# A block inversion in which each partition holds every fourth row, with changed prices in the planner

## The chip, the cores and the metric

The kernel runs on one core of a Trainium2 chip. The metric is device time in microseconds (us) of that core. Of the engines, PE is TensorE (matmuls; PEld is its weight load), DVE is VectorE, ACT is ScalarE, POOL is GpSimd and SP is SyncE, which here issues the DMAs.

## The reference

Two layers on a sequence of 1,024 tokens of width 1,024, all in float32. Layer 1 mixes with a gated DeltaNet (8 heads of 128), layer 2 with stick-breaking attention (8 heads of 128); each is followed by a SwiGLU feed-forward network (FFN, hidden width 2,816) and a gated per-layer embedding. What the change touches is the DeltaNet's triangular system, one per chunk of tokens and head:

```python
G = jnp.cumsum(g, axis=-1)
decay_mat = jnp.exp(jnp.where(causal, G[..., :, None] - G[..., None, :], -jnp.inf))
kk = jnp.einsum('bnhrd,bnhsd->bnhrs', k, k)
a_low = jnp.where(strict, beta[..., None] * kk * decay_mat, 0.0)
rhs = jnp.concatenate([v * beta[..., None], k * (beta * jnp.exp(G))[..., None]], axis=-1)
sol = lax.linalg.triangular_solve(a_low + eye, rhs, left_side=True, lower=True, unit_diagonal=True)
u, w = sol[..., :dv], sol[..., dv:]
...
def step(state, xs):                       # scan over the chunks
    v_new = u_c - w_c @ state
    o = q_c @ state + qk_c @ v_new
    state = state * gl_c + k_c.T @ v_new
```

The kernel uses chunks of 128 tokens, so a head has 8 unit lower triangular matrices of 128 x 128 to invert.

## The kernel before

**Numbers.** Most dense products run as three matmuls on a high and a low part of each float32 operand (`whi`, `wlo`; type float32r), 128 x 128 weights by 512 columns. Splitting weights into the two parts (ACT for `whi`, DVE or POOL for `wlo`) and evacuating PSUM are the main work of the other engines.

**Order.** No loop fixes the order of the instructions. Class `Flow` is a list scheduler that runs while the program is written. Every piece of work is a generator; `run` always resumes the one of best priority whose condition holds at the planned time, and where none can go it takes the next dense matmul from `fill`. After each instruction `issued` advances a model: a clock for each engine, the time at which each tile is written or read last, a price from `cost` for each instruction, one from `lat` for a handover between engines, and for a DMA a landing time (`rings`: its issue + 1.1 us, and bytes at 360 GB/s). A change of any price can so change the order of every later instruction on every engine. The chip then executes each engine's list in that order, and each instruction waits for its inputs. All instructions are issued in the wrapper `Engine.__getattr__`, so the profile gives line 64 for all of them; they are told apart by their tiles.

**Sequence.** Start and first projections up to about 84 us; DeltaNet with dense projections and parts of the embedding products as fill up to about 640 us; output projection; FFN from 785 to 1480 us; attention from 1480 to about 1940 us; output projection; the second FFN to the end.

**The block inversion** (`gdn_inv`, one generator per head `h`). A head's eight 128 x 128 matrices L (tile `LT`) give 8 x 4 = 32 diagonal blocks of 32 x 32 (`B` = 32). They go through DRAM (`Ld`) to tile `Ls`, in which 128 partitions hold the 32 blocks, each block in four neighbouring partitions with all of its 1,024 elements. Each of the four holds `CG` = 8 rows of the block's inverse: tile `xr` (the rows) and `yr` (products), 8 x 32 elements a partition. For s = 30 down to 0 a step multiplies columns s+1 to 31 of the rows by a row of L (`yr<-xr,Ls`) and sums the products into column s (`xr<-yr`), 62 DVE instructions a head. The start values of `xr` and `yr` are unit rows from `masks`, which `const_table` makes. Then `xr` is stored to `Xd` and the blocks are loaded back (`X<-Xd`, four loads) into the diagonal of 128 x 128 matrices, and matmuls (`products`) complete the full inverse `Z`. The next head's `Ls` is loaded only after this head's last step (mark `("x", h)`).

**Around it.** `gdn_prep` makes `QK`, `qf`, `kf`, `vt` per unit (half a head's chunks); it loads `eGb`, a row of decays copied to all partitions, into a tile with one buffer. `Gb` is a load of the same kind. `gdn_rec` is the recurrence over chunks, with tiles `vin`, `vn`, `vE`, `Sm` and PSUM banks `rc`, `r`, `po`. `ple_products` writes embedding products (`<-Z,whi`, `<-ou,whi` in the start) into the banks `po`, `rc`, `r`, `mm`; ACT or DVE clear them into `sg` or `ca`, and these are stored with `ppD<-sg`, `ppD<-ca`. In attention, `z` are scores, `c` their cumulative sums (from `sh`, `sl` by `triR`), `zs` the scores in SBUF, `wh` and `wl` the parts of the weights, and `o` the output.

Of the kernel before, what the change touches and what calls it, by code (L numbers as in the profile page):

```python
# [11 lines left out]
ALU = mybir.AluOpType  # L12
# [3 lines left out]
P = 128  # L16
# [15 lines left out]
B = 32  # L32
NB = P // B
CG = 8
# [3 lines left out]
def const_table():  # L38

    i = np.arange(P)  # L40
    r, c = i[:, None], i[None, :]
    tab = [b.astype(np.float32) for b in (r == c, r <= c, r >= 0 * c, r >= c, r < c)]
    tab.append((r // B > c // B).astype(np.float32))
    g = i[:, None, None] % (B // CG)
    e = np.arange(B)[None, None, :] == CG * g + np.arange(CG)[None, :, None]
    tab += list(e.reshape(P, 2, P).astype(np.float32).transpose(1, 0, 2))
    return np.ascontiguousarray(np.stack(tab, 1))

# [34 lines left out]
class Flow:  # L83
# [30 lines left out]
    def cost(self, eng, op, out, ins, kw):  # L114
        n = 1
        for d in (ins[0] if op == "tensor_reduce" else out).shape[1:]:
            n *= d
        psum = any(x.space == PSUM for x in ins)
        if eng == "pe":
            if op != "transpose" and ins[0].dtype == F32R:  # L120
                return max(n, P) / 2400.0 + 0.0127
            return max(n, P) * (2 if op == "transpose" else 4) / 2400.0 + (0.003 if op == "transpose" else 0.0107)
        if eng == "dve":
            if op == "memset":
                return 0.06 + n / 3840.0
            tail = 0.06 if any(x.shape[-1] == 1 for x in ins) and n > 1 else 0.0
            if any(x.shape[-1] > 1 and x.ap[-1][0] > 1 for x in ins):
                tail += 0.085
            fast = op in ("tensor_copy", "tensor_scalar") and not psum
            return 0.069 + tail + n / (1920.0 if fast else 960.0)  # L130
        if eng == "act":
            us = (0.052 if psum else 0.094) + n / 1200.0
            return us + 0.093 * (len(ins) - 1) + (0.235 if "accum_out" in kw else 0.0)
        if op == "tensor_tensor":
            return 0.295 + 0.166 * n if kw.get("op") == ALU.pow else 0.148 + n * 0.002104
        return 0.4 + n / 1400.0 if op == "affine_select" else 0.1 + n / 1085.0

    def shared(self, eng, op, outs, ins, kw, t, c):

# [22 lines left out]
    def issued(self, eng, op, args, kw):  # L162
        aps = [x for x in list(args) + list(kw.values()) if hasattr(x, "space")]
        if not aps:
            if op == "preload_act_table_set":
                self.table = 3
            return
        outs = [kw["out"] if "out" in kw else aps[0]]
        if "accum_out" in kw:
            outs.append(kw["accum_out"])  # L170
        ins = [x for x in aps if not any(x is o for o in outs)]
        t = self.clock[eng]
        if eng == "pe":
            t = max(t, self.now)
        spans = []
        for x, w in [(o, True) for o in outs] + [(i, False) for i in ins]:
            if x.space == DRAM:
                lo, dims = x.offset, x.ap
            else:
                dims, step = x.ap[1:], x.ap[0][0]  # L180
                lo = x.offset % step if step else x.offset
            hi = lo + 1 + sum((c - 1) * d for d, c in dims)
            rec = self.mem.get(x.name)
            if rec is None:
                rec = self.mem[x.name] = {}
                old = self.old.pop(x.name, None)
                if old is not None and old in self.mem:
                    t = max([t] + [max(v[0] + self.lat(v[1], eng), v[2] + self.lat(v[3], eng)) for v in self.mem.pop(old).values()])
            for (l, h), v in rec.items():
                if l < hi and lo < h:  # L190
                    if not (w and eng == v[1]):
                        t = max(t, v[0] + self.lat(v[1], eng))
                    if (w or x.space == PSUM) and v[3] != eng:
                        t = max(t, v[2] + self.lat(v[3], eng))
            spans.append((rec, (lo, hi), w))
        if eng == "dma":
            n = 4
            for d in outs[0].shape:
                n *= d
            run = min(x.ap[-1][1] if x.ap[-1][0] == 1 else 1 for x in outs + ins)  # L200
            n *= max(1, P // run)
            self.clock["dma"] = t + 0.475
            self.rings = max(self.rings, t + 1.1) + n / 360e3
            end = self.rings
        else:
            c = self.cost(eng, op, outs[0], ins, kw)
            f = [x for x in args if isinstance(x, AF)]
            if f and f[0] in TABLES and TABLES[f[0]] != self.table:
                self.table = TABLES[f[0]]
                t += 1.4  # L210
            if eng in ("dve", "pool"):
                t = self.shared(eng, op, outs, ins, kw, t, c)
            end = t + c
            self.clock[eng] = end
            if eng == "pe":
                self.now = end
        for rec, key, w in spans:
            v = rec.setdefault(key, [-1e9, eng, -1e9, eng])
            if w:
                v[0], v[1] = end, eng  # L220
            elif end > v[2]:
                v[2], v[3] = end, eng
        self.ready = max(self.ready, end + self.LAT[eng])

    def lat(self, a, b):
        if b == "pe":
            return {"pe": 0.0, "dma": 1.2}.get(a, 0.25)
        return 0.13 if a == b and a != "dma" else self.LAT[a]

    def run(self, fill):  # L230
        test = None
# [40 lines left out]
class Net:  # L272
# [679 lines left out]
    def gdn_inv(self, h):  # L952

        nc, flow = self.nc, self.flow
# [37 lines left out]
        rk, rinv, rkb, brk2, rkE, t = (sc[:, i] for i in range(6))  # L992
# [17 lines left out]
        Ld, Xd = self.Ld[h % 2], self.Xd[h % 2]  # L1010
# [8 lines left out]
        for i, u in enumerate(us):  # L1019
            e = slice(4 * i, 4 * i + 4)  # L1020
# [2 lines left out]
        yield  # L1023
        yield lambda: h == 0 or ("x", h - 1) in flow.at
        Ls = self.g("Ls", (P, B * B))
        src = Ld.rearrange("c b s r -> (c b) (s r)").unsqueeze(1).to_broadcast([8 * NB, B // CG, B * B])
        nc.sync.dma_start(Ls, src)

        x = self.g("xr", (P, CG, B))
        y = self.g("yr", (P, CG, B))  # L1030
        rows = self.masks[:, 1:].rearrange("p a (j s) -> p (a j) s", s=B)
        nc.scalar.copy(x[:, :, B - 1], rows[:, :, B - 1])
        nc.scalar.copy(y[:, :, : B - 1], rows[:, :, : B - 1])
        yield
        Lv = Ls.rearrange("p (s r) -> p s r", r=B)
        for s in range(B - 2, -1, -1):
            nc.vector.tensor_tensor(y[:, :, s + 1 :], x[:, :, s + 1 :], Lv[:, s, s + 1 :].unsqueeze(1).to_broadcast([P, CG, B - 1 - s]), op=ALU.mult)
            yield
            nc.vector.tensor_reduce(x[:, :, s], y[:, :, s:], axis=mybir.AxisListType.X, op=ALU.add)
            yield  # L1040
        flow.mark(("x", h))
        nc.sync.dma_start(Xd.rearrange("c b r k -> (c b r k)").rearrange("(p n) -> p n", p=P), x.rearrange("p j s -> p (j s)"))
        yield
        yield lambda: h == 0 or ("w", us[0] - 1) in flow.at
        for b in range(NB):
# [1023 lines left out]
def layout(inputs):  # L2069
# [14 lines left out]

    a = {}
    a["cst"] = const_table()
    a["xT"] = np.ascontiguousarray(g["x"][0].T).reshape(NK, P, S)
    a["pT"] = np.ascontiguousarray(g["p"][:, 0].transpose(0, 2, 1)).reshape(2, 2, P, S)
# [41 lines left out]
```

## Time and profile before

| | us |
|---|---|
| median of 3 runs | 2787.19 (2784.03 to 2788.08) |
| profiled execution, its time | 2787.44 |
| its span in the trace | 2785.7 |
| PE busy | 2741.7 (98%) |
| weight load busy | 2278.1 (82%) |
| DVE busy | 1951.7 (70%) |
| ACT busy | 1324.3 (48%) |
| POOL busy | 860.4 (31%) |

The mean granted clock of PE is 0.996 of full speed. Busy times of different engines overlap. A row of the timeline view gives the start, the duration, the engine, line, operation, output<-inputs, shapes and count, and in brackets how long the engine had idled and what ended that. A row of a group gives total time, then the mean in ns. Queues of SP are written SPq.

### The profile page before, as it was taken

The page shows a single profiled execution, that of the slowest core. Times are in us where ns is not written, and L with a number is a line of the kernel's source. Part 1 is how long each engine was busy: PE and PEld are TensorE (multiplying, and loading weights), DVE is VectorE, ACT ScalarE, POOL GpSimd, SP SyncE. Part 2 cuts the span into 40 slices and gives each one's busy share as a digit, 9 for nine tenths or more (in the row PEclk, how much of TensorE's full clock was granted, in tenths as well). Part 3 has the DMA queues.
Part 4 walks back from the last instruction along what each step waited for, and adds up shares of the span by engine and source line. Part 5 has one row for each costly group of instructions (what it writes and reads, how often), then busy time and mean ns, then how long its engine had stood idle before and what let it go on. Part 6 is the DMA issues. An engine that isn't in the chain of part 4 may idle for free.

```text
span 2785.7 us, 37779 instructions
## 1 busy us (share of the span) xinstructions
PE 2741.7 (98%) x13203; PEld 2278.1 (82%) x13203; DVE 1951.7 (70%) x3733; ACT 1324.3 (48%) x2701; POOL 860.4 (31%) x742
## 2 busy tenths in 40 slices
PE   9999999999999999999999999999999999999999
PEld 8788888888778888888778888888878888888777
DVE  7687887873875665477857778887686565557783
ACT  6655555543433344322335778877443343322241
POOL 0111111100166667444101222221036666643400
PEclk9999999999999999999999999999999999999999
DMA  4412222247334444587232111114514444487623
GB/s 147 143 58 76 75 82 74 74 151 244 140 110 159 155 155 144 223 328 304 106 131 99 54 50 61 54 58 158 200 57 156 150 148 151 144 311 284 262 90 105
DMA packets 165072, 394.85 MB, mean 142 GB/s; under 512 B 34000, under 2 KB 35344, under 8 KB 155408
## 3 DMA queue, kind: packets, MB, share of 16 engines
q1 hardware_dynamic: 164880, 392.43, 39.5%
q8 instruction: 104, 1.70, 0.2%
q14 instruction: 88, 0.72, 0.1%
HBM read 273.77 MB, written 118.59 MB: 141 GB/s over the span
## 4 chain that ended last, share of the span: by engine, by line
PE 86%; DVE 7%; ACT 4%; issue 2%; DMA 1%; POOL 1%; ACTq 0%; POOLq 0%
PE dn L64 38%; PE mm L64 34%; PE tp L64 4%; PE z L64 3%; PE c L64 2%; PE o L64 2%; DVE x L64 1%; PE po L64 1%; PE rc L64 1%; PE r L64 1%; DVE u L64 1%; ACT junk L64 1%; ACT L64 1%; DVE v L64 1%; PE st L64 1%
## 5 line engine op out<-in xcount | busy, mean ns | idle before, releaser
L64 PE MATMUL mm<-x,whi 128*128 128x512 f32 x2848 | 939.0, 400 | 8.7 <-DVE x L64 5.4
L64 PEld LDWEIGHTS mm<-x,whi 128*128 128x128 f32 x2848 | 528.5, 189 | 106.7 <-DVE x L64 7.9
L64 PE MATMUL mm<-x,wlo 128*128 128x512 f32 x1424 | 568.5, 399 | 0.0
L64 PE MATMUL dn<-x,whi 128*128 128x512 f32 x1776 | 548.7, 390 | 1.8 <-DVE x L64 0.9
L64 POOL TENSOR_TENSOR wlo<-raw,whi 128x512 fp32r<-128x512 f32 x236 | 345.5, 1485 | 442.7 <-ACT whi L64 413.2
L64 ACT CAST whi<-raw 128x1024 fp32r<-128x1024 f32 x231 | 242.8, 1051 | 447.4 <-DVE raw L64 244.7
L64 PEld LDWEIGHTS dn<-x,whi 128*128 128x128 f32 x1776 | 333.3, 188 | 73.3 <-DVE x L64 2.6
L64 PE MATMUL dn<-x,wlo 128*128 128x512 f32 x888 | 345.7, 389 | 0.0
L64 PEld LDWEIGHTS mm<-x,wlo 128*128 128x128 f32 x1424 | 269.0, 189 | 46.4 <-issue 0.3
L64 PE MATMUL dn<-hx,whi 128*128 128x512 f32 x864 | 267.4, 390 | 0.4 <-DVE hx L64 0.2
L64 DVE TENSOR_TENSOR tt<-u,tt 128x512 fp32r<-128x512 f32 x140 | 143.9, 1028 | 81.5 <-ACT tt L64 81.5
L64 PEld LDWEIGHTS dn<-x,wlo 128*128 128x128 f32 x888 | 166.7, 188 | 34.4
L64 PEld LDWEIGHTS dn<-hx,whi 128*128 128x128 f32 x864 | 162.8, 189 | 35.0 <-DVE hx L64 0.6
L64 DVE TENSOR_TENSOR v<-v,dn 128x512 f32<-128x512 f32 x112 | 76.5, 684 | 155.4 <-PE dn L64 155.0
L64 DVE TENSOR_TENSOR wlo<-raw,whi 128x512 fp32r<-128x512 f32 x226 | 153.9, 693 | 27.2 <-ACT whi L64 26.9
L64 PE MATMUL dn<-hx,wlo 128*128 128x512 f32 x432 | 169.1, 391 | 3.4 <-POOL wlo L64 3.4
L64 POOL TENSOR_TENSOR wlo<-sw,whi 128x512 fp32r<-128x512 f32 x102 | 144.3, 1431 | 2.0 <-ACT whi L64 2.0
L64 ACT CAST tt<-u 128x512 fp32r<-128x512 f32 x140 | 84.8, 619 | 123.5 <-DMA yD<-tt 100.2
L64 DVE TENSOR_TENSOR E<-E,dn 128x512 f32<-128x512 f32 x132 | 90.0, 684 | 71.4 <-PE dn L64 69.1
L64 POOL TENSOR_TENSOR rs<-ms,nhalf 128x4 f32<-128x4 f32 x11 | 12.3, 1122 | 330.7 <-DVE ms L64 330.7
L64 PE MATMUL dn<-y,whi 128*128 128x512 f32 x352 | 108.4, 389 | 0.0
L64 DVE SCALAR_TENSOR_TENSOR ca<-xe,conv,ca 128x512 f32<-128x512 f32 x144 | 106.2, 744 | 0.9 <-ACT ca L64 0.4
(376 smaller groups left out, 5124.8 us busy)
## 6 DMA issues: line engine op xcount, KB each, us to landing
yD<-tt SPq DMA_DIRECT2D x296, 256.0 KB, 2.4
x<-yD SPq DMA_DIRECT2D x58, 1024.0 KB, 11.3
raw<-f_s SPq DMA_DIRECT2D x84, 512.0 KB, 3.7
raw<-d_s SPq DMA_DIRECT2D x40, 512.0 KB, 5.9
raw<-w_in SPq DMA_DIRECT2D x33, 512.0 KB, 4.0
hx<-yD SPq DMA_DIRECT2D x16, 1024.0 KB, 14.5
x<-oD SPq DMA_DIRECT2D x26, 512.0 KB, 5.8
raw<-g_out SPq DMA_DIRECT2D x16, 512.0 KB, 5.2
```

The source lines that it names most:

```text
L64: r = issue(*args, **kw)
```

## The change

- **Layout.** The four copies of a block now lie 32 partitions apart: partition p belongs to block p mod 32, and with g = p // 32 it holds rows g, g+4, g+8 and so on. `const_table` makes the unit rows for this.
- **Fewer elements.** At step s only rows that reach past column s have anything to sum. With interleaved rows these are the last 8 - j of each partition, j = (s + 1) // 4, and multiply and sum run over these alone. The count of instructions stays.
- **Ls.** Its load runs over the four copies outermost, then 32 blocks, then 1,024 elements; before it was 32 blocks, four copies, 1,024 elements.
- **Start values.** ACT copies the 256 elements of `masks` to `xr` and to `yr` (before 8 and 248 of them).
- **Xd.** It is stored by four DMAs of 32 partitions in pieces of 128 bytes, instead of one DMA of 1 KB per partition.
- **Prices.** A short f32r matmul costs at least 0.1 us (before 0.066 at 128 columns), POOL's tensor_tensor a little more, affine_select less (0.252 instead of 0.491 us at 128 elements), a DMA whose source repeats over partitions (`Gb`, `eGb`, and by its new address list `Ls`) lands 2.5 us instead of 1.1 us after issue beside its bytes, and DVE hands over to itself in 0.06 instead of 0.13 us.

```diff
-    g = i[:, None, None] % (B // CG)
-    e = np.arange(B)[None, None, :] == CG * g + np.arange(CG)[None, :, None]
+    g = i[:, None, None] // (8 * NB)
+    e = np.arange(B)[None, None, :] == g + B // CG * np.arange(CG)[None, :, None]
...
-                return max(n, P) / 2400.0 + 0.0127
+                return max(n / 2400.0 + 0.0127, 0.1)
...
-            return 0.295 + 0.166 * n if kw.get("op") == ALU.pow else 0.148 + n * 0.002104
-        return 0.4 + n / 1400.0 if op == "affine_select" else 0.1 + n / 1085.0
+            return 0.295 + 0.166 * n if kw.get("op") == ALU.pow else 0.169 + n * 0.002125
+        return 0.119 + n / 960.0 if op == "affine_select" else 0.1 + n / 1085.0
...
+            spread = any(x.ap[0][0] == 0 for x in ins)
             self.clock["dma"] = t + 0.475
-            self.rings = max(self.rings, t + 1.1) + n / 360e3
+            self.rings = max(self.rings, t + (2.5 if spread else 1.1)) + n / 360e3
...
-        return 0.13 if a == b and a != "dma" else self.LAT[a]
+        return {"dve": 0.06, "dma": self.LAT["dma"]}.get(a, 0.13) if a == b else self.LAT[a]
...
-        src = Ld.rearrange("c b s r -> (c b) (s r)").unsqueeze(1).to_broadcast([8 * NB, B // CG, B * B])
+        src = Ld.rearrange("c b s r -> (c b) (s r)").unsqueeze(0).to_broadcast([B // CG, 8 * NB, B * B])
...
-        nc.scalar.copy(x[:, :, B - 1], rows[:, :, B - 1])
-        nc.scalar.copy(y[:, :, : B - 1], rows[:, :, : B - 1])
+        nc.scalar.copy(x, rows)
+        nc.scalar.copy(y, rows)
...
-            nc.vector.tensor_tensor(y[:, :, s + 1 :], x[:, :, s + 1 :], Lv[:, s, s + 1 :].unsqueeze(1).to_broadcast([P, CG, B - 1 - s]), op=ALU.mult)
+            j = (s + 1) // (B // CG)
+            nc.vector.tensor_tensor(y[:, j:, s + 1 :], x[:, j:, s + 1 :], Lv[:, s, s + 1 :].unsqueeze(1).to_broadcast([P, CG - j, B - 1 - s]), op=ALU.mult)
...
-            nc.vector.tensor_reduce(x[:, :, s], y[:, :, s:], axis=mybir.AxisListType.X, op=ALU.add)
+            nc.vector.tensor_reduce(x[:, j:, s], y[:, j:, s:], axis=mybir.AxisListType.X, op=ALU.add)
...
-        nc.sync.dma_start(Xd.rearrange("c b r k -> (c b r k)").rearrange("(p n) -> p n", p=P), x.rearrange("p j s -> p (j s)"))
+        xd = Xd.rearrange("c b (j g) k -> g (c b) j k", g=B // CG)
+        for g in range(B // CG):
+            nc.sync.dma_start(xd[g], x[g * 8 * NB : (g + 1) * 8 * NB])
```

The set of PE's matmuls and the counts of DVE, ACT and POOL instructions stay the same. SP issues 24 more stores of Xd, and 3 more DMAs because one attention output is spilled to DRAM instead of being taken over directly. PE's order is the same up to the start of the DeltaNet, in the first FFN, and from the end of attention on.

Three places of the order follow; a row gives the line, operation, output<-inputs and output shape, names with running numbers. First, SP's queue where the first head's `Ls` and the two `eGb` are loaded, before:

```order
L64 DMA Ld_92<-LT_915 32x8x32 x4
L64 DMA Ls_983<-Ld_92 128x1x1024
L64 DMA eGb_989<-gD 128x512
L64 DMA eGb_996<-gD 128x512
L64 DMA ppD<-sg_974 128x512
L64 DMA raw_1069<-w_in 128x1024
L64 DMA ppD<-sg_1060 128x512
```

and now:

```order
L64 DMA Ld_92<-LT_913 32x8x32 x4
L64 DMA Ls_984<-Ld_92 128x1x1024
L64 DMA eGb_990<-gD 128x512
L64 DMA eGb_997<-gD 128x512
L64 DMA ppD<-sg_972 128x512
L64 DMA ppD<-sg_1065 128x512
L64 DMA raw_1083<-w_in 128x1024
```

Ls, both eGb and the first store keep their places; only a weight load (`raw`) and a store change places behind them.

Second, DVE in the same place, from the last piece of work ahead of the first step of the inversion to the reader of the first `eGb`, before:

```order
L64 TENSOR_TENSOR wlo_951<-raw_790,whi_950 128x512
L64 TENSOR_TENSOR yr_986<-xr_985,Ls_983 128x8
L64 TENSOR_REDUCE xr_985<-yr_986 128x8
L64 SCALAR_TENSOR_TENSOR QK_1025<-tp_172_1008,sc_815,Gb_724 128x128 x4
L64 SCALAR_TENSOR_TENSOR ca_965<-xe_910,conv,ca_965 128x512
L64 SCALAR_TENSOR_TENSOR ca_970<-xe_948,conv,ca_970 128x512
L64 TENSOR_TENSOR wlo_951<-raw_790,whi_950 128x512
L64 TENSOR_TENSOR yr_986<-xr_985,Ls_983 128x8x2
L64 SCALAR_TENSOR_TENSOR QK_1036<-tp_174_1018,sc_815,Gb_725 128x128 x4
L64 TENSOR_TENSOR qf_601<-qf_601,eGb_989 128x512
```

and now:

```order
L64 TENSOR_TENSOR wlo_937<-raw_795,whi_936 128x512
L64 SCALAR_TENSOR_TENSOR QK_1024<-tp_172_1009,sc_816,Gb_721 128x128 x4
L64 TENSOR_TENSOR yr_987<-xr_986,Ls_984 128x1
L64 TENSOR_REDUCE xr_986<-yr_987 128x1
L64 TENSOR_TENSOR yr_987<-xr_986,Ls_984 128x2
L64 SCALAR_TENSOR_TENSOR QK_1037<-tp_174_1019,sc_816,Gb_722 128x128 x4
L64 SCALAR_TENSOR_TENSOR ca_969<-xe_894,conv,ca_969 128x512
L64 SCALAR_TENSOR_TENSOR ca_976<-xe_964,conv,ca_976 128x512
L64 TENSOR_TENSOR wlo_937<-raw_795,whi_936 128x512
L64 TENSOR_REDUCE xr_986<-yr_987 128x1
L64 TENSOR_TENSOR qf_601<-qf_601,eGb_990 128x512
```

The first four QK updates went ahead of the first step, which has 1 x 1 elements a partition where it had 8 x 1; the reader of eGb stays behind the first steps.

Third, PE at the end of attention, from the last `z` of 128 x 128 on (`mm` is fill), before:

```order
L64 MATMUL z_3650_18777<-qh_18524,kl_18321 128x128
L64 MATMUL o_18563<-wh_18788,vh_18105 128x512
L64 MATMUL o_18563<-wl_18790,vh_18105 128x512
L64 MATMUL o_18563<-wh_18788,vl_18106 128x512
L64 MATMUL z_3658_18803<-qh_18524,kh_18320 128x256
L64 MATMUL z_3658_18803<-ql_18525,kh_18320 128x256
L64 MATMUL z_3658_18803<-qh_18524,kl_18321 128x256
L64 MATMUL c_3659_18807<-sh_18797,triR 128x128
L64 MATMUL c_3659_18807<-sl_18801,triR 128x128
L64 MATMUL c_3659_18807<-sh_18797,triR 128x128
L64 MATMUL c_3659_18807<-sl_18801,triR 128x128
L64 MATMUL mm_18534<-x_18204,whi_18322 128x512 x2
```

and now:

```order
L64 MATMUL z_3653_18812<-qh_18586,kl_18347 128x128
L64 MATMUL mm_18596<-x_18236,whi_18348 128x512
L64 MATMUL z_3659_18834<-qh_18586,kh_18346 128x256
L64 MATMUL z_3659_18834<-ql_18587,kh_18346 128x256
L64 MATMUL z_3659_18834<-qh_18586,kl_18347 128x256
L64 MATMUL c_3660_18838<-sh_18829,triR 128x128
L64 MATMUL c_3660_18838<-sl_18832,triR 128x128
L64 MATMUL mm_18596<-x_18236,whi_18348 128x512
L64 MATMUL mm_18596<-x_18236,wlo_18349 128x512
L64 MATMUL mm_18629<-x_18236,whi_18444 128x512
L64 MATMUL c_3660_18838<-sh_18829,triR 128x128
L64 MATMUL c_3660_18838<-sl_18832,triR 128x128
```

The three `o` products that stood behind this z now stand ahead of its three matmuls (not in the rows), and single fill products stand between z and the `c` products.

## The prediction

> **What bounds the kernel now.** I read the page's first lines, then a table of stretches, then the idle times in front of matmuls, then the rows of the inversion.
>
> ```profile
> span 2785.7 us, 37779 instructions
> PE 2741.7 (98%) x13203; PEld 2278.1 (82%) x13203; DVE 1951.7 (70%) x3733; ACT 1324.3 (48%) x2701; POOL 860.4 (31%) x742
> PE 86%; DVE 7%; ACT 4%; issue 2%; DMA 1%; POOL 1%; ACTq 0%; POOLq 0%
> ```
>
> PE is busy for 98% of the span and carries 86% of the chain that ended last. The change gives PE the same matmuls of the same sizes. So only the 44 us in which PE idles, the stretches of lower clock, and new waits can move the time; fewer DVE elements are worth nothing by themselves.
>
> ```profile
> 84.00:116.00 32.00, 26.22 (x145) 21.56 (x145) 21.80 (x80) 22.47 (x68) 3.70 (x4) 1.00 0.40 135
> 116.00:640.00 524.00, 520.26 (x3043) 442.07 (x3042) 407.39 (x1197) 285.52 (x809) 52.55 (x66) 1.00 0.28 89
> 785.00:1480.00 695.00, 689.25 (x3058) 569.28 (x3057) 453.85 (x642) 244.18 (x339) 327.20 (x233) 1.00 0.50 183
> 1480.00:1930.00 450.00, 449.79 (x2251) 375.09 (x2250) 353.81 (x744) 347.60 (x852) 91.59 (x152) 1.00 0.22 74
> 1930.00:1945.00 15.00, 13.18 (x52) 10.62 (x51) 11.57 (x25) 9.97 (x21) 2.68 (x5) 0.77 0.21 74
> ```
>
> Columns: stretch, length, busy time of PE, weight loads, DVE, ACT, POOL, then PE's clock, DMA share, GB/s. The new order touches the DeltaNet (84 to 640) and attention (1480 to 1945); the FFN of 785 to 1480 and everything behind 1945 keep their matmul order. In the touched stretches PE idles 32.00 - 26.22 = 5.8, then 3.7, 0.2 and 1.8 us, and the last one runs at clock 0.77, worth another (1 - 0.77) x 15 = 3.5 us. That is 15 us: no gain can be larger. The DVE of the DeltaNet is busy 407 of 524 us, PE 520.
>
> ```profile
> PE r L64 <- ACT sg L64: 3.5, 1, 3.5
> PE mm L64 <- ACT ca L64: 1.8, 1, 1.8
> 92.36 1.16 PE L64 MATMUL tp<-qf,kf 128*128 128x128 f32 x8 [0.47 <-ACT vt L64]
> 103.72 0.50 PE L64 MATMUL r<-Z,whi 128*128 128x512 f32 x1 [3.52 <-ACT sg L64]
> 112.24 0.50 PE L64 MATMUL mm<-Z,whi 128*128 128x512 f32 x1 [1.78 <-ACT ca L64]
> 1934.27 0.50 PE L64 MATMUL o<-wh,vh 128*128 128x512 f32 x1 [1.05 <-DVE wh L64]
> 1935.00 0.79 PE L64 MATMUL o<-wl,vh 128*128 128x512 f32 x1 [0.23 <-DVE wl L64]
> 1937.56 0.47 PE L64 MATMUL c<-sh,triR 128*128 128x128 f32 x1 [0.38 <-DVE zs L64]
> ```
>
> The first two rows are the longest waits of PE between 84 and 640 us (total, times, longest); the others are where they and the attention's waits lie. Nearly all idle time in question is at the first head's start and at the end of attention.
>
> **The start, 84 to 116 us.** Why does PE wait 3.52 us for a copy?
>
> ```profile
> 90.28 8.32 SPq L64 DMA_DIRECT2D eGb<-gD  x2
> 93.11 0.18 DVE L64 TENSOR_TENSOR yr<-xr,Ls 128x8 f32<-128x8 f32 x1 [3.23 <-DMA Ls<-Ld]
> 98.70 0.39 SPq L64 DMA_DIRECT2D ppD<-sg  x1
> 102.45 0.69 DVE L64 TENSOR_TENSOR qf<-qf,eGb 128x512 f32<-128x512 f32 x1 [2.73 <-DMA eGb<-gD]
> 103.08 0.59 ACT L64 COPY sg<-r 128x512 f32<-128x512 f32 x1 [3.08 <-DMA ppD<-sg]
> ```
>
> SP holds the second load of eGb until DVE has read the first (8.32 us), the store of sg is queued behind it on SP, ACT waits for that store before it may refill sg, and PE waits for ACT to clear bank r. DVE is late because the first multiply of the inversion waited 3.23 us for Ls. The new SP order has the same sequence Ld, Ls, eGb, eGb, stores, so I leave this wait as it is. Ahead of the first multiply now stand four QK updates, but eGb's reader is still behind it. The wait at 112.24 goes, since the copies of ca and sg there are ordered anew, and something of that kind comes back. Value -1; ends: -4.0 (1.78, 0.47 and half of 3.52 go), +3 (Ls comes 4 us later, see below, less the four QK updates that now run ahead of it).
>
> **The inversion's DVE work.**
>
> ```profile
> L64 DVE TENSOR_TENSOR yr<-xr,Ls x248: 160/292/726, 93.1 to 595.0; 128x8 f32<-128x8 f32 x4, 128x24 f32<-128x24 f32 x4, 128x40 f32<-128x40 f32 x4, 128x56 f32<-128x56 f32 x4
> L64 DVE TENSOR_REDUCE xr<-yr x248: 157/296/423, 93.4 to 595.6; 128x8 f32<-128x16 f32 x4, 128x8 f32<-128x32 f32 x4, 128x8 f32<-128x48 f32 x4, 128x8 f32<-128x64 f32 x4
> L64 DVE TENSOR_REDUCE xr<-yr 128x8 f32<-128x256 f32 x1 | 0.4, 411 | 0.0
> L64 DVE TENSOR_REDUCE xr<-yr 128x8 f32<-128x24 f32 x1 | 0.2, 180 | 0.0
> L64 ACT COPY yr<-masks x8: 395/402/407, 90.9 to 553.9; 128x248 f32<-128x248 f32 x8
> ```
>
> The count stays 2 x 248; the elements per partition fall from 8,184 to 5,720 in a head, 19,712 in eight. From 24 to 256 elements a reduce goes from 180 to 411 ns, 1.0 ns per element: some 20 us less DVE work between 93 and 596 us. None is on PE's path except where DVE is late. The same element formula stood in the planner before, so it has already put other work there; worth 0. The two start copies on ACT become 256 elements each; the x copy grows by at most 0.4 us a head, on an engine that is busy 286 of 524 us and before Ls lands: 0.
>
> **The load of Ls.** Its source had each block's row four times running; now the four copies are the outermost step of the address list.
>
> ```profile
> L64 SPq DMA_DIRECT2D Ls<-Ld x8: 524/525/590, 89.6 to 554.5; - x8
> DMA to landing us min/median/max: 3.3/3.4/3.4
> 91.60:92.60 1.00, 0.53 (x5) 0.33 (x4) 0.00 (x0) 1.00 (x5) 0.00 (x0) 1.00 0.93 367
> 129.41 0.33 SPq L64 DMA_DIRECT2D Xd<-xr  x1
> 129.79 0.55 SPq L64 DMA_DIRECT2D Ls<-Ld  x1
> 133.47 0.17 DVE L64 TENSOR_TENSOR yr<-xr,Ls 128x8 f32<-128x8 f32 x1 [4.09 <-DMA Ls<-Ld]
> 211.67 0.53 SPq L64 DMA_DIRECT2D Ls<-Ld  x1
> 215.70 0.17 DVE L64 TENSOR_TENSOR yr<-xr,Ls 128x8 f32<-128x8 f32 x1
> ```
>
> All eight loads land 3.4 us after issue. No load of before has so short an outermost step, so both ends are worked out. Lower end 0: it lands after 3.4 us as now. Upper end: the shape uses only four of the 16 DMA engines. At 91.6 us 367 GB/s at 0.93 busy make 24.7 GB/s per engine; 524,288 bytes are then 1.3 us on 16 and 5.3 us on four, and it lands after 3.4 + 4.0 = 7.4 us. The new price (2.5 instead of 1.1 us) puts the first multiply 1.4 us later, where now it stands 4.0 us behind the issue (211.67 to 215.70): 5.4, so DVE would wait 2 us in each of seven heads. At 133.47 a DVE wait of 4.09 us brought PE no idle time at all, so I let half reach PE: 7 x 2 x 0.5 = 7 us. Value +2, nearer to the measured 3.4.
>
> The Trainium skill, "DMA: Bandwidth & Descriptors", section "Rules for kernel authors", speaks against the change: an outermost dimension of c < 16, its example a leading zero-stride broadcast, confines a DMA to at most c engines. By it the landing would be 7.4 us and the sum 5 us higher; by the rows of before, 0. No load there tests it.
>
> The store of Xd becomes four issues of 32 partitions. At 0.33 us each Ls and the four loads X behind it on SP start 1 us later a head. The planner charges every issue, and what waits for X are transposes that the plan puts behind its landing: 0. The 128-byte pieces (1,024 a head) add to DMA busy shares of 0.28: 0.
>
> **The prices.** The f32r matmul, POOL and select prices only change the plan; what they did to it is seen in the order. The one that I count is DVE's handover to itself, 0.06 instead of 0.13 us.
>
> ```profile
> 107.29 0.23 DVE L64 TENSOR_TENSOR yr<-xr,Ls 128x72 f32<-128x72 f32 x1
> 107.56 0.24 DVE L64 TENSOR_REDUCE xr<-yr 128x8 f32<-128x80 f32 x1
> 107.83 0.24 DVE L64 TENSOR_TENSOR yr<-xr,Ls 128x80 f32<-128x80 f32 x1
> 490.61 0.34 DVE L64 TENSOR_SCALAR vE<-r,sc 128x128 f32<-128x128 f32 x1
> 491.00 0.30 PEld L64 LDWEIGHTS rc<-vE,kt 128*128 128x128 f32 x2 [0.18 <-DVE vE L64]
> 491.08 0.41 PE L64 MATMUL rc<-vE,kt 128*128 128x128 f32 x2
> ```
>
> Dependent steps follow each other every 0.27 us. The old price of such a step was 0.069 + 80/960 + 0.13 = 0.28, the new one 0.21: the plan now thinks DVE early by 0.06 us per adjacent dependent pair. A handoff of the recurrence has little cover: vE ends at 490.95 and its matmul starts at 491.08. In the new DVE order some 27 handoffs stand behind 2 to 7 such pairs (4.5 x 0.06 - 0.15 of cover = 0.12 us each, 3 us in all) and six behind 13 to 32 (20 x 0.06 - 0.15 = 1.0 each, 6 us); most have none in front. Ends 0 (DVE resynchronises on other waits ahead) and +9; value +2, because most handoffs lie at the lower end. What is late then is the next rc or r product on PE, and all behind it.
>
> **Old small waits** of 116 to 640 (3.7 us) are drawn anew by a new order: ends -3.7 and +2, value -1.
>
> **End of attention.** Before, the three o products at 1934 and the c products at 1937 follow each other with little fill; now single fill products stand between the last z and c. Ends -5.1 (1.05 + 0.23 + 0.38 and the 3.5 of clock), 0 (the o products still come right behind their softmax weights). Value -2: the short waits go, the clock drop half the time.
>
> The Trainium skill, "TensorE: Matmul & The Clock Gate", section "HAM oscillation — how this bites in real kernels", gives PE idle gaps of over about 3.4 us as what lowers the clock. The trace differs: the 3.52 us gap before 103.72 lies in a stretch at 1.00, and the 1.05 us gap at 1934 in one at 0.77. By the rule the tail term would be -1.7 at most, by the rows -5.1.
>
> **Sum.** 2787.44 (the profiled run; span 2785.7) - 1 + 2 + 2 - 1 - 2 = 2787.4. The median of the three runs is 0.25 us lower, so 2787. Some 0.2% (5.6 us) is what a measurement of this kernel can tell from no change: faster is below 2781.6, slower above 2792.8.
>
> **Rivals.**
> R1, slower: Ls on four engines. It decides once the landing takes over about 6 us from issue. Ls +7 instead of +2, and at the start DVE comes 3 us later to eGb's reader, so +1 instead of -1: 2787.4 + 5 + 2 = 2794. For it: the new outermost step of four, and that PE's wait at 103.72 hangs on the same DVE chain. Against it: eight landings of 3.4, a 4.09 us wait that cost nothing.
> R2, faster: the better prices remove waits. Start -4.0, tail -5.1, old waits -1, Ls and handover 0: 2777. For it: the waits at 112.24 and 1934 are single places that the order changes. Against it: the SP sequence that makes the 3.52 us is the same.
> R3, slower by the handover price alone: +9 instead of +2: 2794. Against it: the counts of pairs in front of handoffs are mostly zero.
> That the inversion's elements don't fall in cost, since the shapes have fewer rows, would show on DVE and not in the time: PE is not waiting for it.
>
> **How the numbers follow.** Forecast 0.42 (own range 2782 to 2793; 0.04 faster, 0.35 same, 0.03 slower), R1 0.25 (0.07 same, 0.18 slower), R2 0.24 (0.20 faster, 0.04 same), R3 0.09 (0.03 same, 0.06 slower). Faster 0.24, same 0.49, slower 0.27. The range goes to R2 below, 2778, and above to R1 with half of the remaining handover end, 2794 + 4 = 2798.
>
> **What would show it.** Right: PE busy within 3 us of 2741.7; yr and xr rows down by 20 us; PE's wait for sg near 103 us still 3 to 4 us; no wait for ca near 112; no clock below 0.9 in 1930 to 1945; Ls landing below 5 us and DVE idle for Ls under 8 us in total. Ls landing near 7.4 and DVE idle for it of 15 us or more is R1. Waits of PE for vE, vin or Sm summing to over 5 us between 116 and 640 with Ls landing at 3.4 is R3. I am wrong altogether if a new wait of over 5 us appears in attention, whose order changes although none of its operations do, or if the untouched FFN stretches move.

## The result, and the profile after

The changed kernel takes 2851.2 us (median of 4 runs, 2849.0 to 2854.7) against 2787.6 us: a ratio of 1.0232, 95% interval 1.0214 to 1.0250. It is 64 us slower; the prediction said 2787, its range ended at 2798, and even its slow rival R1 stood at 2794. A few executions in the comparisons below were slow (one took 5.6 ms); the ratios leave them out, the medians do not.

The page after, in the lines that answer to those shown of before:

```profile
span 2847.3 us, 37860 instructions
PE 2758.2 (97%) x13203; PEld 2283.6 (80%) x13203; DVE 1933.8 (68%) x3733; ACT 1325.0 (47%) x2701; POOL 866.3 (30%) x742
PE 76%; DVE 10%; DMA 6%; issue 4%; ACT 2%; SPq 1%; POOL 1%; POOLq 0%; DVEq 0%; ACTq 0%
PE dn L64 36%; PE mm L64 28%; PE tp L64 3%; PE z L64 3%; PE c L64 2%; DMA Ls<-Ld 2%; PE o L64 2%; DVE x L64 1%; SPq L64 1%; DMA raw<-d_s 1%; PE po L64 1%; DVE xr L64 1%; DVE yr L64 1%; DVE ca L64 1%; DVE wlo L64 1%
```

DVE is 18 us less busy, as the change intends. PE's share of the chain fell from 86 to 76%, and the load of Ls, which was no link worth a row before, now carries 2% of the span by itself. The same stretches as before, columns as in the prediction:

```profile
84.00:116.00 32.00, 23.21 (x116) 18.78 (x116) 21.29 (x78) 20.06 (x63) 2.45 (x2) 0.89 0.32 107
116.00:640.00 524.00, 485.56 (x2754) 409.72 (x2753) 368.46 (x1133) 266.82 (x750) 50.42 (x65) 0.96 0.24 71
785.00:1480.00 695.00, 682.11 (x2998) 561.06 (x2998) 466.08 (x660) 247.49 (x345) 349.05 (x246) 0.99 0.49 176
1480.00:1930.00 450.00, 449.79 (x2214) 371.85 (x2212) 340.90 (x696) 321.53 (x770) 84.81 (x131) 1.00 0.20 69
84.00:660.00 576.00, 527.17 (x2965) 443.54 (x2965) 402.29 (x1242) 295.24 (x839) 54.86 (x69) 0.96 0.25 75
```

In 116 to 640 us PE gets through 2,754 matmuls where it did 3,043. Over the whole span PE idles 2847.3 - 2758.2 = 89.1 us instead of 2785.7 - 2741.7 = 44.0, and it is busy 16.5 us longer with the same matmuls. These 45.1 and 16.5 us are the 61.6 us by which the span grew. Most of it is lost in the DeltaNet: from 84 to 660 us PE idles 576.0 - 527.2 = 48.8 us, 39 more than the 5.8 + 3.7 = 9.5 of before, and the clock there is 0.96 instead of 1.00, which would be at most 0.04 x 576 = 23 us if PE were busy all the time. What the idle time is, by PE's waits in that stretch (total, times, longest) and DVE's:

```profile
PE r L64 <- DVE vin L64: 13.5, 4, 5.8
PE tp L64 <- DMA X<-Xd: 7.9, 4, 5.9
PE r L64 <- ACT sg L64: 6.9, 1, 6.9
PE po L64 <- ACT ou L64: 5.9, 2, 3.1
PE r L64 <- DVE xr L64: 5.1, 1, 5.1
PE rc L64 <- DVE xr L64: 4.9, 1, 4.9
DVE yr L64 <- DMA Ls<-Ld: 46.5, 8, 8.2
```

The names in PE's rows differ from head to head, since whichever operation stands behind the blocked DVE comes late. DVE's row names the cause: 46.5 us of waiting for Ls, once in each of the eight heads. Before it was 7.6 us in three, by the view of that tile:

```profile
  DMA Ls<-Ld: 7.6, 3
```

One head of the changed kernel in full, SP's, DVE's and PE's rows of the timeline:

```profile
296.86 0.56 SPq L64 DMA_DIRECT2D Ls<-Ld  x1
306.98 0.16 DVE L64 TENSOR_TENSOR yr<-xr,Ls 128x1 f32<-128x1 f32 x1 [5.26 <-DMA Ls<-Ld]
307.48 0.35 DVE L64 TENSOR_SCALAR vE<-r,sc 128x128 f32<-128x128 f32 x1
307.88 0.80 PE L64 MATMUL rc<-vE,kt 128*128 128x128 f32 x2 [4.92 <-DVE xr L64]
```

and the stretch around it in the table of stretches:

```profile
305.00:313.00 8.00, 5.12 (x15) 4.26 (x16) 4.83 (x23) 3.67 (x12) 2.33 (x4) 0.57 0.24 80
```

Ls is issued at 296.86 and lets DVE go at 306.98, 10.1 us later. The recurrence's vE is queued behind the first step on DVE, and PE, which needs vE, idles 4.92 of the 5.26 us. In the 8 us around it the clock of PE averages 0.57 (last row). Why the load takes so long shows in a window before the next DMA is issued (the last two columns are DMA share and GB/s), after:

```profile
229.40:230.50 1.10, 1.10 (x8) 0.92 (x7) 1.10 (x3) 1.10 (x5) 0.00 (x0) 1.00 0.26 97
```

and before:

```profile
213.10:214.30 1.20, 1.20 (x8) 1.07 (x7) 0.35 (x1) 0.65 (x4) 0.00 (x0) 1.00 0.94 369
```

Busy share 0.26 of 16 engines is four engines, at 97 GB/s; before it was 0.94, or nearly all of them, at 369 GB/s. The rate of one engine is about the same (97/4 = 24 GB/s; 369/15 = 25).

In the last head SP issues no other DMA between Ls and the first step:

```profile
604.68 0.57 SPq L64 DMA_DIRECT2D Ls<-Ld  x1
615.43 0.35 SPq L64 DMA_DIRECT2D raw<-w_proj  x1
613.51 0.16 DVE L64 TENSOR_TENSOR yr<-xr,Ls 128x1 f32<-128x1 f32 x1 [3.16 <-DMA Ls<-Ld]
607.00:612.00 5.00, 5.00 (x30) 4.03 (x29) 1.48 (x5) 2.73 (x7) 0.00 (x0) 1.00 0.27 87
```

Alone it takes 8.8 us, at 0.27 busy and 87 GB/s. In the other heads it takes 9.4 to 10.9 us.

### The profile page after: what moved, and what is told of

It is laid out like the page before. It is cut to its first block, busy times and chain, and to the rows that moved or that the text cites. A ratio compares the mean times of both kernels' runs of the same rounds, so it can differ in the third digit from the quotient of the medians.

```text
span 2847.3 us, 37860 instructions
## 1 busy us (share of the span) xinstructions
PE 2758.2 (97%) x13203; PEld 2283.6 (80%) x13203; DVE 1933.8 (68%) x3733; ACT 1325.0 (47%) x2701; POOL 866.3 (30%) x742
## 4 chain that ended last, share of the span: by engine, by line
PE 76%; DVE 10%; DMA 6%; issue 4%; ACT 2%; SPq 1%; POOL 1%; POOLq 0%; DVEq 0%; ACTq 0%
PE dn L64 36%; PE mm L64 28%; PE tp L64 3%; PE z L64 3%; PE c L64 2%; DMA Ls<-Ld 2%; PE o L64 2%; DVE x L64 1%; SPq L64 1%; DMA raw<-d_s 1%; PE po L64 1%; DVE xr L64 1%; DVE yr L64 1%; DVE ca L64 1%; DVE wlo L64 1%
## 5 line engine op out<-in xcount | busy, mean ns | idle before, releaser
L64 DVE TENSOR_TENSOR tt<-u,tt 128x512 fp32r<-128x512 f32 x140 | 136.4, 974 | 82.0 <-ACT tt L64 81.8
```

What stands on the lines that cost most here:

```text
L64: r = issue(*args, **kw)
```

## The experiments

The comparisons are ratios to the kernel before with their 95% intervals; times are medians.

**1. The load alone (wide).** The plan is told of the changed kernel's one DMA, so every engine keeps the order of the changed kernel.

```diff
-        nc.sync.dma_start(Ls, src)
+        blocks = Ld.rearrange("c b s r -> (c b) (s r)")
+        for g in range(B // CG):
+            self.tc.nc.sync.dma_start(Ls[g * 8 * NB : (g + 1) * 8 * NB], blocks)
+        flow.issued("dma", "dma_start", (Ls, src), {})
```

> The changed kernel with one edit: Ls is loaded by four DMAs of 32 partitions, each from the 32 blocks directly, instead of one DMA with the four copies outermost. The planner is told of the one old DMA, so the order on every engine stays that of the changed kernel. Theory 1 (the load uses four of 16 DMA engines and lands about 10 us after issue; DVE waits at the first step of each inversion, PE waits for DVE, and each such gap halves PE's clock for some us): Ls lands 4 to 5 us after issue, DVE's waits for Ls fall from 46.5 us to under 12, the half-clock windows between 100 and 640 us go (8 now, 44 us long), and the time is 2780 to 2793. Theory 2 (the new prices, above all the DVE handover of 0.06 us, make a plan that is too tight, and PE waits for DVE whatever the load takes): the time stays above 2825, PE keeps waiting 3 to 6 us a head for vin, vE and ou.

Measured 2803.1 us, 1.0059 (1.0046 to 1.0072). The stretch of the DeltaNet, and what DVE waited for in the view of Ls:

```profile
116.00:640.00 524.00, 512.22 (x2984) 431.44 (x2982) 387.78 (x1176) 282.46 (x798) 51.69 (x66) 1.00 0.28 86
```

```profile
  DMA Ls<-Ld: 5.7, 4
```

DVE's wait for Ls falls to 5.7 us, the clock in this stretch is back at 1.00, PE idles 11.8 us there instead of 38.4. With the order kept and only this load changed, the narrow load cost 1.0232 - 1.0059, some 48 us. But 16 us are left, above the 2780 to 2793 of theory 1, and far below the 2825 of theory 2.

**2. The prices alone (prices_only).** The kernel before with the five new prices.

> The kernel before with the new prices alone; layout, elements, Ls load and Xd store as before. Theory 1: 2781 to 2793, since Ls lands after 3.4 us. Theory 2: above 2825. The prediction's own terms (handover +2, old waits -1, end of attention -2, start -2) make 2785.

Measured 2812.7 us, 1.0094 (1.0079 to 1.0108). Between both theories: without the load and without the layout the prices cost 26 us.

**3. The layout with the old prices (layout_old_prices).**

> The changed kernel with the old prices: new layout, fewer elements, Ls with the four copies outermost. The plan has the first step of the inversion 1.4 us earlier behind the load. Theory 1: as slow as the changed kernel or slower, 2848 to 2870 (up to 1.4 us more in each of eight heads). Theory 2: near 2790.

Measured 2847.3 us, 1.0217 (1.0203 to 1.0232). Theory 1 holds for the load: DVE waits 61.2 us for Ls here, more than the 46.5 of the changed kernel, since the plan has the first step earlier. But the kernel is not slower for it. Either the other new prices cost about what the later first step saves, or the new order hides it; this run does not tell which.

**4. The load priced as slow as it is (ls_priced).**

```diff
+            if spread and ins[0].ap[0][1] == B // CG:
+                end = t + 7.0 + n / 360e3
```

> The changed kernel with one more price: a source with four copies outermost lands 7.0 us after issue beside its bytes (instead of 2.5), so that the plan has the first step of each inversion about 9.5 us behind the load. The load is as slow as in the changed kernel. Theory 1: DVE gets other work in the meantime, its waits for Ls fall below 15 us and the time to 2785 to 2805; what is left above 2787 is the price of the longer chain per head. Theory 2: above 2825, since the handover price is kept.

Measured 2819.3 us, 1.0122 (1.0106 to 1.0138), above the range. DVE's waits for Ls fall to 8.1 us as expected, and 31 us come back. It is still 16 us behind wide, whose load really is fast. Half of that is one wait, since the plan can hide that DVE waits, but not that the first inversion ends later. A row of its timeline, where the first X is needed:

```profile
141.82 1.09 PE L64 MATMUL tp<-cst,X 128*128 128x128 f32 x4 [8.31 <-DMA X<-Xd]
```

PE waits 8.31 us for X there, 5.9 us at most in the changed kernel. The rest of the 16 us is not taken apart; the order of this run is also a new one (see 6).

**5. Two engines instead of four (ls_k2).** Order as in the changed kernel; Ls by two DMAs with two copies outermost each.

```diff
-        nc.sync.dma_start(Ls, src)
+        half = Ld.rearrange("c b s r -> (c b) (s r)").unsqueeze(0).to_broadcast([2, 8 * NB, B * B])
+        for g in range(2):
+            self.tc.nc.sync.dma_start(Ls[g * 64 : g * 64 + 64], half)
+        flow.issued("dma", "dma_start", (Ls, src), {})
```

> The changed kernel, order unchanged, with Ls loaded by two DMAs of 64 partitions, each with two copies outermost. If the outermost count sets how many of the 16 engines work: both use two engines, 524,288 bytes take 10 us or more of transfer instead of 5, Ls lands 15 us or more behind issue, and the time is 2880 to 2920 (5 us more in each of eight heads, and more time at half clock). If the load is slow for another reason (a source that is read four times, a repeated address), two copies a DMA are no slower than four: 2835 to 2855.

Measured 2892.2 us, 1.0381 (1.0367 to 1.0395). One head in the timeline, and DVE's waits for all:

```profile
238.88 1.11 SPq L1030 DMA_DIRECT2D Ls<-Ld  x2
254.09 0.16 DVE L64 TENSOR_TENSOR yr<-xr,Ls 128x1 f32<-128x1 f32 x1 [9.58 <-DMA Ls<-Ld]
```

```profile
DVE yr L64 <- DMA Ls<-Ld: 85.2, 8, 12.4
```

Ls comes 15.2 us after issue, DVE waits 85.2 us, and the time lies in the range that was set for an outermost count that decides (2880 to 2920). Two copies outermost are slower than four; the load of before and the four DMAs of wide, which read each block four times as well, are fast: it is the outermost count, not the repeated source.

**6. The prices one by one (p_handover, p_matmul, p_rest) and a control (jitter_a).** All on the kernel before.

> The kernel before with one new price alone: DVE hands over to itself in 0.06 instead of 0.13 us (and ACT, POOL and SP to themselves as before). New prices together cost 26 us on that kernel. Theory A (the handover price is the one that hurts: the plan takes DVE for earlier than it is): 2800 to 2815. Theory B (no price is wrong in itself, but the order before was a lucky draw among many, and any other draw loses some us): 2790 to 2805, like the other two. Theory C (the price of short matmuls hurts): 2782 to 2793.

> The kernel before with one new price alone: an f32r matmul costs at least 0.1 us. Theory A: 2782 to 2793. Theory B: 2790 to 2805. Theory C: 2800 to 2815.

> The kernel before with the other new prices: POOL's tensor_tensor, affine_select, and 2.5 us for a DMA whose source repeats over partitions (in this layout Gb and eGb, not Ls). Theories A and C: 2782 to 2793. Theory B: 2790 to 2805.

> A control: the kernel before with the handover of an engine to itself priced at 0.128 instead of 0.13 us, which means nothing but redraws the order (1,267 of PE's rows differ, against 1,822 with the new handover price). Theory A and C: 2782 to 2793. Theory B: slower than before by 5 us or more, as any redraw.

| kernel | us | ratio (95%) |
|---|---|---|
| p_handover | 2810.4 | 1.0078 (1.0061 to 1.0095) |
| p_matmul | 2785.5 | 0.9995 (0.9985 to 1.0005) |
| p_rest | 2797.7 | 1.0035 (1.0023 to 1.0047) |
| jitter_a | 2795.1 | 1.0025 (1.0015 to 1.0034) |

Theory C falls. The control is the surprise: a price changed by 2 ns, which says nothing new about the chip and only redraws the order, costs 8 us. So p_rest, with 10 us, is no evidence against its prices; and p_matmul, a redraw as well, costs nothing. The handover price costs three times as much as the control; theory A fits the difference, theory B the rest. In 116 to 640 us, the control:

```profile
116.00:640.00 524.00, 518.08 (x3023) 439.40 (x3021) 406.51 (x1194) 284.24 (x806) 54.39 (x66) 1.00 0.28 89
```

and p_handover:

```profile
116.00:640.00 524.00, 509.36 (x2944) 424.97 (x2943) 402.61 (x1179) 276.56 (x782) 51.79 (x67) 1.00 0.27 83
```

The control gets through 20 matmuls fewer than the 3,043 of before, p_handover 99 fewer, with 14.6 us of PE idle instead of 3.7. Some of PE's waits in p_handover, from 84 to 640 us:

```profile
PE tp L64 <- ACT vf L64: 3.0, 3, 1.3
PE po L64 <- ACT ou L64: 2.8, 4, 1.0
PE rc L64 <- DVE vE L64: 1.1, 2, 0.8
PE r L64 <- DVE vin L64: 1.1, 2, 0.8
```

Those for DVE's vE, vin and Sm (0.3) make 2.5 us, less than the 5 us by which the prediction would have known R3; those for ACT's vf, ou and vn (2.5) make 8.3.

**7. Luck or bias (jitter_b, h_0062, h_016).** A second control, a second draw of the low handover price, and a price that is too high.

> A second control: the kernel before with a DMA priced at 1.12 instead of 1.1 us behind its issue, which means nothing but redraws the order (470 of PE's rows differ; 1,267 in the first control, 888 with the price of short matmuls). If any redraw costs: 2789 to 2800. If the first control was an accident: 2782 to 2789.

> The kernel before with DVE's handover at 0.062 us, a second draw of the price of 0.06 (2810). If that price is biased and so harmful: 2803 to 2816. If 2810 was the luck of one order: anywhere from 2787 to 2800, as the controls.

> The kernel before with DVE's handover at 0.16 us, as far to the other side of the 0.12 us that the trace shows as half of the way to 0.06. If a plan that has DVE too early is what harms: no harm beyond a redraw, 2784 to 2797. If any wrong price harms in the same way: 2800 or more.

jitter_b 2795.1 us, 1.0032 (1.0020 to 1.0043); h_0062 2808.9 us, 1.0081 (1.0067 to 1.0095); h_016 2801.7 us, 1.0049 (1.0034 to 1.0065). A second control costs 9 us, as the first did 8. The low price gives the same 22 us in a second, different order (2,966 matmuls in 116 to 640 us, where p_handover has 2,944). So it harms in itself, by 12 to 14 us beyond the redraws that cost 8 to 10, as far as two orders can show it. The high price meets the range that was set for "any wrong price harms" (2800 or more), but its interval overlaps that of the second control, so whether a price that is too high harms as well stays open.

**8. The layout without the load's fault (layout_wide_old, wide_old_handover, wide_matmul_price).** All three are wide with prices put back: all of them, the handover alone, all but that of short matmuls.

> The layout alone: the changed kernel with the old prices and with Ls loaded by four DMAs of 32 partitions (the plan sees one). If the load cost what the changed kernel lost and the handover price most of the rest: 2778 to 2793, where fewer DVE elements (19,712, some 20 us of DVE) can only help at single waits. If the layout itself harms (four stores of Xd, four loads of Ls on SP, larger start copies): 2795 or more, with PE waiting for X.

> The changed kernel with Ls loaded by four DMAs (2803 as measured) and the handover price alone put back to 0.13 us. If the handover price is what hurts: 2784 to 2796. If it is the draw of an order: within 5 us of 2803.

> The new layout with Ls loaded by four DMAs and of the new prices only that of short matmuls, which cost nothing on the kernel before. As layout_wide_old, 2775 to 2793; a candidate to beat both kernels.

2794.3 us, 1.0033 (1.0020 to 1.0046); 2794.7 us, 1.0039 (1.0026 to 1.0052); 2792.6 us, 1.0030 (1.0018 to 1.0041). Putting the handover price back takes 6 to 8 us off wide's 2803, less than on the kernel before, and the intervals of the two just overlap. None beats the kernel before, and the layout by itself is 9 us slower with its own order.

**9. The layout in the order of before (layout_same_order, rows_in_place, rows_two_queues).** The new instructions are issued, but the planner is told of the old shapes, so each engine has exactly the old order. In the first, Ls and Xd take four DMAs each. In the second the partitions stay as they were and Ls is loaded by the one old DMA. The third issues two of the four stores of Xd from ACT:

```diff
-    e = np.arange(B)[None, None, :] == CG * g + np.arange(CG)[None, :, None]
+    e = np.arange(B)[None, None, :] == g + B // CG * np.arange(CG)[None, :, None]
...
+        xd = Xd.rearrange("c b (j g) k -> g (c b) j k", g=B // CG)
+        for g in range(B // CG):
+            (raw.sync, raw.scalar)[g % 2].dma_start(xd[g], x[g :: B // CG])
```

> The new layout with fewer elements, Ls by four DMAs and Xd by four DMAs, but the planner is told of the old shapes, so that every engine has the order of the kernel before (only the shapes of the inversion's instructions and the pieces of Ls and Xd differ). If the 8 us of the layout alone (2794 with its own order) come from the redrawn order: 2778 to 2788, no slower than before. If they come from the layout's work (four stores, four loads, copies): 2792 to 2797.

> Order and partition layout of the kernel before (a block in four neighbouring partitions, Ls loaded by the one old DMA), but each partition holds every fourth row and the steps leave out the short rows; Xd is stored by four DMAs, each from every fourth partition, and the plan sees one. Against layout_same_order (2793, +6) this takes away the four loads of Ls alone. If the four stores of Xd, 0.6 us of SP each, make those 6 us (PE waits 5.1 us for X there): 2789 to 2794, PE still waiting for X in some heads. If the split load of Ls made them: 2779 to 2787, at or below before.

> As rows_in_place, but two of the four stores of Xd are issued by ACT's queue, beside the two on SP. If the issue time of the stores on SP is what makes X late: the waits for X shrink by half or more and the time is 2 to 4 us below rows_in_place, 2780 to 2789, a candidate to beat the kernel before. If the 128-byte pieces are what makes X late: the same as rows_in_place. If ACT, held by the store's wait for DVE, becomes late for PE: slower than rows_in_place.

2793.4 us, 1.0023 (1.0013 to 1.0032); 2791.9 us, 1.0023 (1.0014 to 1.0032); 2791.3 us, 1.0016 (1.0007 to 1.0024). With the old order and some 17 us less DVE work the kernel is 4 to 6 us slower than before, and the split load of Ls isn't the reason. The stores are the likely one. The store's group before and in rows_in_place, and the largest of PE's waits there:

```profile
L64 SPq DMA_DIRECT2D Xd<-xr x8: 319/320/327, 129.4 to 596.1; - x8
L1050 SPq DMA_DIRECT2D Xd<-xr x32: 521/606/658, 130.4 to 602.7; - x32
```

```profile
PE tp L64 <- DMA X<-Xd: 5.5, 6, 2.3
```

A store of 128-byte pieces takes SP 0.61 us against 0.32 us for the one old store, four of them 2.4 us a head, and X then comes late: PE waits 5.5 us for it in six places, where before it did not wait. With two queues that wait is 2.9 us, but the time is the same within its interval, so how the 4 to 6 us divide between the stores' issue time and the rest is not settled.

Of the 64 us, then, the narrow load makes 48. Of the 16 that wide has left, the handover price makes 6 to 8. The other 8 to 10 are as much as layout_wide_old loses with the old prices (9), and as much as a redraw alone, so the layout's own share in them is not separated. The 4 to 6 us of experiment 9 can't simply be added: there the plan knew of one store, while wide's plan charges all four, and PE waits only 1.3 us for X.

## Why the prediction was wrong, point by point

- **The load of Ls** is the step that failed: +2 where it measured some 48 us. The mechanism was there as R1, four of 16 engines (0.26 of the engines busy), but its price of +7 was far too low as well. The Trainium skill, "DMA: Bandwidth & Descriptors", section "Rules for kernel authors", states that an outermost dimension of a size c below 16 confines a DMA to at most c engines; this trace agrees with 0.26 of the 16 engines busy. What failed in R1 were three sizes, and the choice between the ends:
  - The landing was worked out as 7.4 us; it took 10.1 in the head shown and 8.8 to 10.9 in the eight. Other loads that follow at once (Gb at 297.52) can explain only a part, since the last head's load took 8.8 us with no other DMA issued. Why that is 1.4 us more than bytes and latency make stays open.
  - The share that reaches PE was set at one half after a single row, 133.47, where PE did not idle at all. It was four fifths: against wide, 46.5 - 5.7 = 40.8 us more of DVE's waits for Ls came with 48.8 - 15.7 = 33.1 us more idle time of PE from 84 to 660 us. In the head shown it was 4.92 of 5.26 us.
  - The lower clock behind the waits was given no term, although the prediction had used the row of 1930 to 1945, where 1.8 us of idle time came with 0.77. PE was busy 16.5 us longer, where the prediction's sign of being right was 3.
  - Choosing between 0 and 7 the value near the measured 3.4 us of landing was wrong too: those eight rows belonged to the old address list and spoke for nothing in the new one.
- **The handover price**: direction right, size wrong, mechanism not shown. +2 with an end of +9; alone it cost 22, of which a redraw may explain 8 to 10. The waits for vE, vin and Sm, by which it was to act, were 2.5 us in p_handover; through which others it costs the rest stays open. The trace of the changed kernel shows the price to be wrong at the smallest steps as well:

```profile
237.43 0.16 DVE L64 TENSOR_TENSOR yr<-xr,Ls 128x1 f32<-128x1 f32 x1 [4.09 <-DMA Ls<-Ld]
237.62 0.15 DVE L64 TENSOR_REDUCE xr<-yr 128x1 f32<-128x2 f32 x1
237.81 0.16 DVE L64 TENSOR_TENSOR yr<-xr,Ls 128x2 f32<-128x2 f32 x1
```

  A step comes every 0.19 us; the old price is 0.069 + 1/960 + 0.13 = 0.20, the new one 0.13. The prediction counted only pairs directly in front of a handoff.
- **Old waits drawn anew**: -1, ends -3.7 and +2. Two controls that only redraw the order cost 8 and 9 us. Below that lay the assumption that a new draw is as good as the old; the old order was better than every other draw of the kernel before that was run but one (p_matmul, the same). The reason is not shown.
- **The store of Xd**: costed at 0 with 0.33 us an issue, since the planner charges every issue. It takes 0.61, and where the plan knew of one store PE waited 5.1 and 5.5 us for X (layout_same_order, rows_in_place). Where the plan charged all four and Ls was fast, that wait was 0.6 to 1.3 us, no more than in kernels with the one store (0 to 1.6), so the 0 was nearly right there. In the changed kernel it was 7.9 us, with Ls late.
- **The start**: the wait for sg stayed and grew to 6.9 us, the +3 of the upper end; the wait for ca at 112 went, as said. It was the upper end because Ls was late: with the fast load of wide the wait for sg was 2.1 us.
- **End of attention**: wrong. In the changed kernel the o products behind the last weights wait longer than before:

```profile
1997.99 0.49 PE L64 MATMUL o<-wh,vh 128*128 128x512 f32 x1 [1.75 <-DVE wh L64]
1998.72 0.80 PE L64 MATMUL o<-wl,vh 128*128 128x512 f32 x1 [0.23 <-DVE wl L64]
1993.00:2008.00 15.00, 11.26 (x44) 8.75 (x42) 9.37 (x20) 7.22 (x16) 1.50 (x4) 0.77 0.35 126
```

  The single fill products went behind z, and the wait is ahead of the o products, which the new order puts in front of z: the order was read at the wrong side of the wait. The clock drop is there as before, 0.77 over 15 us, only later in the span.
- **Right**: fewer DVE elements are worth nothing by themselves (18 us less DVE, no run faster for it), the price of short matmuls costs nothing, and Ls on four engines is what the list of signs named: DVE idle for it of 15 us or more (46.5).

## What to carry to other kernels

A rewritten access pattern of a DMA is a new transfer: here the outermost count (2, 4 or 32) decided how fast it went, so price it from that count, and not from landings of the old pattern. A wait on an engine that feeds the bound can reach the bound for the greater part (here four fifths) and cost again through its clock. Where a planner orders the work, run a control with a meaningless change of a price before judging a meaningful one: here a redraw alone cost up to 0.3%.

## What the runs showed of the hardware

- Shares of DMA engines by the outermost count: four copies outermost 0.26 busy and 97 GB/s, 32 blocks outermost 0.94 and 369 GB/s. The 512 KB came 8.8 to 10.9 us after issue with four, 3.4 us with 32, and 15.2 us in the head shown with two.
- Clock: in the changed kernel a gap of 4.92 us was followed by some us at about half clock (0.57 over 8 us). The length of one gap does not decide it: 3.52 us in the kernel before came with 1.00 in 84 to 116 us, 3.61 us at the same place in jitter_a with 0.95, and 1.05 us at 1934 with 0.77 in 1930 to 1945.
- The issue of one DMA on SP took 0.61 us in 128-byte pieces of 32 partitions (rows_in_place), and 0.32 us for 128 pieces of 1 KB (before).
